# Four PSUM banks for the large products, one for the recurrence's first operand and its state update

## Chip, cores and metric

One core of one Trainium2 chip. The metric is device time in microseconds (us) of one execution. The kernel is written with tiles: the source sets no waits, they are derived from which instructions write and read a tile, and a tile with a tag takes one of the buffers of that tag (`bufs`, 1 where nothing is said). A buffer is taken again only when everything that used it has finished. PE, VectorE (DVE), ScalarE (ACT) and GpSimd (POOL) each run their own instructions in one fixed order.

## Reference

One layer over 1024 prompt tokens and 8 sample tokens (1032 columns, `TS`), width 2048, all in float32:

```python
mod = silu(c) @ w_ada + b_ada                     # shift, scale, gate
h = rmsnorm(x, norm_g) * (1 + sc) + sh
p_all = concat([shift_prev, h]) @ w_in            # 2048 x 10368
o_s, ... = s5_branch(u, z_s5, ...)                # state-space branch, GELU, GLU, SiLU(z)
o_r, wkv = rwkv_branch(cur, prev, z_rw, ...)      # 16 heads of 64; per token:
#   sa = S @ -kk;  S = S * d + outer(sa, b) + outer(v, k);  o = S @ r
#   then groupnorm, + sum(r * k * r_k) * v (bonus), times silu(z)
mixed = sigmoid(g_s5) * (o_s @ w_out[:1024]) + sigmoid(g_rw) * (o_r @ w_out[1024:])
y = rmsnorm(x + gt * mixed, final_g)
```

## The kernel before

Channels lie on partitions, tokens on the free axis. A large product is a *job*: 128 columns of a weight against all tokens, in three groups of some 344 tokens. Weights and activations are split into a high and a low float16 half, so one group is 3 x 16 matmuls (3 x 8 for the last weights) into one PSUM tile `pg` (L455, tag `g`, three banks). The group's evacuation by ScalarE and VectorE depends on the job: u L535, z of S5 (`zt`) L552/L553, r, k, v of the recurrence (`ZB`) and its low-rank input (`LW`) L511 to L517, z of the recurrence (`Z`) L567/L568, gates L587, output L1504. Next to it VectorE and ScalarE prepare the next job's weights: absolute maximum (L157), high half `whi` (L405), low half `wlo` (L406).

All other work is a set of Python generators that a driver (`Driver.slot`) steps between every eight matmuls, by estimated costs. This makes the order of the source; each engine's final order follows it, but an instruction whose inputs come late can stand behind later ones.

The recurrence (RWKV) runs over eight pairs of heads, 0 to 7, in chunks of 64 tokens. For each pair:
- `rw_prep` makes the decays and keys, with small products `pml` (L651) and `pmk` (L665) in the two `pm` banks; `rw_operands` makes the chunk matrices (`pma`, L737).
- `rw_side` transposes operands and makes the bonus term: three products `pmb` (L778), each read by VectorE (L779) into `BV`. Their tiles have the tags xp, sp, up. The jobs for the next pair's k and v need this step in the source's order, so it is issued at once ahead of them.
- `rw_tinv` inverts 16 triangular 64 x 64 matrices on VectorE by forward substitution, 63 steps of L798 and L800, writes the result to DRAM (`dT`, L804) and loads it back as `TT` (L808).
- `rw_chain` has 16 steps k. A step: `xp` = AR·S + M·VN (L826, L827); VectorE copies one half of the partitions to `XS` (L828), ScalarE the other to `XR` (L829); `up` = TT·XS (L834), VectorE makes `UB` of it (L835); `sp` = KN·VN + BN·UB (L837, L839); VectorE makes the next state `S` (L842); `up`'s second half (L840) and `XR` give the output `ON` (L845). xp, sp and up are a bank each.
- `rw_tail` normalizes and writes the pair's output to DRAM.

So the eight PSUM banks are: g 3, pm 2, xp, sp, up. The modulation products (`pmod` in `mod_block`, at the start; `pmg` in `gt_mod`, near the end) alternate over xp and sp, and the small transposing products behind them (`pmt`, `pmh`) use up. In the S5 stage `pmy` (L1290) needs `XRt`, a copy of the scan's states.

In PE's order the first step of a pair's chain begins early: L827 and L837 of k = 0 stand among the products for the next pair's v, and L834 of k = 0, which needs TT, behind those for its r.

Of the kernel before, what the change touches and what calls it, by code (L numbers as in the profile page):

```python
# [11 lines left out]
F32 = mybir.dt.float32  # L12
# [49 lines left out]
G3 = [(0, 344), (344, 688), (688, TS)]  # L62
# [68 lines left out]
class Hybrid:  # L131
# [79 lines left out]
    def mod_block(self, col, stage, row, out, xload=None):  # L211

        nc, d = self.nc, self.d
        self.mtog = 1 - getattr(self, "mtog", 0)
        q = self.ps.tile([128, 512], F32, name="pmod", tag=("xp", "sp")[self.mtog])
        for j in range(8):
            wa = stage(j)
            nc.sync.dma_start(wa, d["w_ada"][256 * j:256 * j + 256, col:col + 512].rearrange("(k p) n -> p k n", p=128))
            if xload is not None and j % 2:
                xload()  # L220
            self.mod_step(q, self.cs32, wa, 2 * j)
            yield (0, 600, 0)
        nc.scalar.copy(row, q)
        yield (0, 0, RGAP)
        q2 = self.ps.tile([128, 4, 16], F32, name="pmt", tag="up")
        for i in range(4):
            nc.tensor.matmul(q2[:, i, 0:9], row[:, 128 * i:128 * i + 128], self.sel, start=True, stop=True)
        out(q2)
        yield (300, 1000, 0)
# [197 lines left out]
    def run_jobs(self, jobs):  # L427

        nc, drv = self.nc, self.drv
        for i, job in enumerate(jobs):  # L430
            if job.need is not None:
                drv.force(lambda: job.need in self.flags)
            if job.before is not None:
                job.before()
            if job.bind is not None:
                job.bind()
            nxt = jobs[i + 1] if i + 1 < len(jobs) else None
            ws = None
            if nxt is not None:
                if nxt.ahead:  # L440
                    drv.force(lambda: nxt.known)
                ws = self.weights(nxt, jobs[i + 2] if i + 2 < len(jobs) else None)
                drv.bgs.insert(0, [ws, 0.0, 1.0])
            if i == 0:
                self.product_by_rows(job)
            for acc in job.accs if i else []:
                w_ = acc.job or job
                for g0, g1 in acc.groups:
                    q = self.ps.tile([128, 512], F32, name="pg", tag="g", bufs=3)
                    w = g1 - g0  # L450
                    n = 0
                    tot = 3 * len(acc.kts)
                    for wk, rk in acc.kts:
                        for a, b in ((w_.hi, acc.hi), (w_.hi, acc.lo), (w_.lo, acc.hi)):
                            nc.tensor.matmul(q[:, :w], a[:, wk, :], b[:, rk, g0:g1], start=(n == 0), stop=(n == tot - 1))  # L455
                            n += 1
                            if n % SLOT == 0 and n < tot:
                                drv.slot(SLOT * (w / 2.4 + 2.5))
                    v = acc.evac(q, g0, g1)
                    drv.slot(SLOT * (w / 2.4 + 2.5), v or 0.0)  # L460
            if nxt is not None:
                drv.force(lambda: getattr(nxt, "split", False))
            if job.done is not None:
                job.done()

    def product_by_rows(self, job):

        acc = job.accs[0]
        qs = [self.ps.tile([128, 512], F32, name="pg", tag="g", bufs=3) for _ in acc.groups]
        n = len(acc.kts)  # L470
        for i, (wk, rk) in enumerate(acc.kts):
            for q, (g0, g1) in zip(qs, acc.groups):
                for j, (a, b) in enumerate(((job.hi, acc.hi), (job.hi, acc.lo), (job.lo, acc.hi))):
                    self.nc.tensor.matmul(q[:, :g1 - g0], a[:, wk, :], b[:, rk, g0:g1], start=(i == j == 0), stop=(i == n - 1 and j == 2))
            self.drv.slot(1300, 0)
        for q, (g0, g1) in zip(qs, acc.groups):
            acc.evac(q, g0, g1)
# [274 lines left out]
    def rw_side(self):  # L752

        nc, c = self.nc, self.c
        V = nc.vector
        for p in range(8):
            while f"ops{p}" not in self.flags or (p and f"o{p - 1}" not in self.flags):
                yield None
            ON = self.ON.rearrange("p a t -> p (a t)")
            BV = self.BV[:, :T]  # L760
            n = 0
            for t, dst, W in ((5, self.BN, ON), (2, self.KN, BV), (7, self.VN, ON)):
                V.transpose(out=W, in_=self.z(t)[:, :T])
                yield (1150, 0, 0)
                W3 = W.rearrange("p (c b j) -> p c b j", c=16, b=2)
                for h in range(2):
                    for a in range(2):
                        for b in range(2):
                            p0 = 64 * h + 32 * a
                            d0 = 64 * h + 32 * b  # L770
                            f = nc.scalar.copy if n % 3 else nc.gpsimd.tensor_copy
                            f(dst[d0:d0 + 32, :, p0:p0 + 32], W3[p0:p0 + 32, :, b, :])
                            n += 1
                yield (0, 0, BGAP if t == 7 else 2000)
            RK, Vv = self.z(6), self.z(7)
            for (g0, g1), tag in zip(G3, ("xp", "sp", "up")):
                q = self.ps.tile([128, 512], F32, name="pmb", tag=tag)
                nc.tensor.matmul(q[:, :g1 - g0], c["bd"], RK[:, g0:g1], start=True, stop=True)  # L778
                V.tensor_tensor(out=self.BV[:, g0:g1], in0=q[:, :g1 - g0], in1=Vv[:, g0:g1], op=ALU.mult)  # L779
                yield (450, 578, PBG)  # L780
            nc.gpsimd.tensor_copy(self.SMP[:, 6, p, :], self.BV[:, T:TS])
            self.flags.add(f"side{p}")
# [29 lines left out]
    def rw_chain(self, p):  # L812
# [3 lines left out]
        for k in range(16):  # L816
# [4 lines left out]
            mb = self.M[:, k, 0:64] if e == 0 else self.M[:, k, 128:192]  # L821
            xs = self.XS[e]
            g = GC[:, k:k + 1]
            xp = self.ps.tile([128, 128], F32, name="xp", tag="xp")
            if k:
                nc.tensor.matmul(xp, self.AR[:, a, 128 * e:128 * e + 128], S0, start=True, stop=False)  # L826
            nc.tensor.matmul(xp, mk, self.VN[:, k, :], start=(k == 0), stop=True)  # L827
# [5 lines left out]
            up = self.ps.tile([128, 2, 128], F32, name="up", tag="up")  # L833
            nc.tensor.matmul(up[:, 0, :], self.TT[:, a, :], xs, start=True, stop=True)  # L834
            V.scalar_tensor_tensor(out=self.UB, in0=up[:, 0, :], scalar=-1.0, in1=c["bd"], op0=ALU.mult, op1=ALU.mult)  # L835
            sp = self.ps.tile([128, 128], F32, name="sp", tag="sp")
            nc.tensor.matmul(sp, self.KN[:, k, :], self.VN[:, k, :], start=True, stop=False)  # L837
            yield (200, 436, CG[1])
            nc.tensor.matmul(sp, self.BN[:, k, :], self.UB, start=False, stop=True)  # L839
# [510 lines left out]
    def gt_mod(self, st):  # L1350

        nc, d, c = self.nc, self.d, self.c
        V = nc.vector
        pool = self.pool("gtp", stack=st)
        small = lambda nm, *s, **k: pool.tile([128] + list(s), k.get("dt", F32), name=nm, tag=nm, bufs=k.get("bufs", 1))
        while "ysplit" not in self.flags:
            yield None
        cs32 = self.cond(pool)
        yield (300, 0, 2000)

        def load(n):
            w = []
            for h in range(2):
                t = self.ot.tile([128, 8, 128], F32, name="gw", tag="xres")
                nc.scalar.dma_start(t, d["w_ada"][1024 * h:1024 * h + 1024, 2 * DM + 128 * n:2 * DM + 128 * n + 128]
                                    .rearrange("(k p) n -> p k n", p=128))
                w.append(t)
            return w

        for n in range(16):  # L1370
            while n >= GQ and f"out{n - GQ}" not in self.flags:
                yield None
            w = load(n)
            yield (0, 0, 6000)
            q = self.ps.tile([128, 128], F32, name="pmg", tag=("xp", "sp")[n % 2])
            for h in range(2):
                self.mod_step(q, cs32, w[h], 8 * h)
            row = small("grow", 128)
            nc.scalar.copy(row, q)
            yield (0, 1300, 6000)  # L1380
            q2 = self.ps.tile([128, 16], F32, name="pmh", tag="up")
            nc.tensor.matmul(q2[:, 0:9], row, self.sel, start=True, stop=True)
            V.tensor_scalar(out=self.gt[:, n, :], in0=q2[:, 0:9], scalar1=c["b_ada"][:, 32 + n:33 + n], scalar2=None, op0=ALU.add)
            yield (200, 250, 0)
            self.flags.add(f"gt{n}")
            yield (0, 0, HGAP)
# [401 lines left out]
```

## Time and profile before

| | |
|---|---|
| median of 3 runs | 2989.96 us (2986.49 to 2994.73) |
| profiled execution | 2995.25 us |
| its span, first to last instruction | 2993.4 us |
| mean granted clock of TensorE | 0.961 of full speed |
| PE busy | 2735.1 us (91%) |
| VectorE busy | 2038.6 us (68%) |
| ScalarE busy | 1104.7 us (37%) |
| DMA, mean over the span | 101 GB/s |

A wait is the idle time of an engine just before an instruction, with what ended it. An engine's idle time costs only where the end of the kernel hangs on it. Matmuls overlap one another, so that one of 0.31 us takes PE some 0.145 us.

### The profile page before, as it was taken

What the parts mean: (1) busy time and instruction counts of PE and PEld (TensorE: products, weight loads), DVE (VectorE), ACT (ScalarE), POOL (GpSimd) and SP (SyncE); (2) the same over time, 40 slices, a digit from 0 to 9 for tenths busy, and PEclk for the clock granted to TensorE, in tenths of its full rate; (3) what the DMA queues carried; (4) which work ended last, traced back from release to release, by engine and by line L of the source; (5) the groups of instructions that cost most, each with busy time, mean ns of one, the idle gap of its engine ahead of it and who ended that gap; (6) DMA issues with size and microseconds to landing.
All of it is one profiled execution on the core that took longest, in us unless ns stands there. A gap on an engine that the chain in (4) does not pass through costs nothing.

```text
span 2993.4 us, 47028 instructions
## 1 busy us (share of the span) xinstructions
PE 2735.1 (91%) x18330; PEld 1819.5 (61%) x18330; DVE 2038.6 (68%) x5106; ACT 1104.7 (37%) x1934; POOL 189.8 (6%) x386
## 2 busy tenths in 40 slices
PE   5689989999989999899899899998999898999997
PEld 1156656666657666567566566575676665666664
DVE  5579788753676766855856856767667865656665
ACT  2143223333434344254254254253352145522321
POOL 1100000010100100000001001001000000000002
PEclk7799999999999999999999999999999999999998
DMA  9834443331321313123213212212222337574443
GB/s 334 270 73 90 88 71 92 95 87 49 65 63 48 81 51 78 52 64 82 57 44 77 71 47 74 60 52 66 62 72 70 106 131 258 164 239 142 141 142 128
DMA packets 434735, 301.82 MB, mean 101 GB/s; under 512 B 115184, under 2 KB 400016, under 8 KB 433232
## 3 DMA queue, kind: packets, MB, share of 16 engines
q1 hardware_dynamic: 398224, 281.19, 33.7%
q10 hardware_dynamic: 36128, 17.33, 2.1%
q8 instruction: 144, 2.36, 0.3%
q14 instruction: 79, 0.65, 0.1%
q0 software_dynamic: 160, 0.30, 0.0%
HBM read 241.44 MB, written 57.32 MB: 100 GB/s over the span
## 4 chain that ended last, share of the span: by engine, by line
PE 45%; DVE 26%; DMA 14%; issue 8%; ACT 4%; POOL 1%; SPq 1%; ACTq 0%; DVEq 0%; POOLq 0%
PE pg L455 33%; DMA ws<-w_in 4%; DMA od<-BV 4%; DVE TM L798 4%; DVE ZB L800 4%; DVE wlo L406 3%; PE pma L737 2%; DVE wam L157 2%; DMA wa<-w_ada 2%; PE up L840 1%; PE sp L839 1%; PE pmod L236 1%; PE up L834 1%; ACT whi L405 1%; DMA TT<-dT 1%
## 5 line engine op out<-in xcount | busy, mean ns | idle before, releaser
L455 PEld LDWEIGHTS <-whi 128*128 128x128 f16 x9600 | 945.5, 99 | 563.8 <-issue 113.0
L455 PE MATMUL pg<-H,whi 128*128 128x344 f16 (+2 forms) x3840 | 1202.2, 313 | 74.4 <-DVE ZB L517 42.7
L455 PE MATMUL pg<-H,wlo 128*128 128x344 f16 (+2 forms) x3840 | 1202.0, 313 | 0.0
L455 PE MATMUL pg<-HL,whi 128*128 128x344 f16 (+2 forms) x3840 | 1201.9, 313 | 0.0
L455 PEld LDWEIGHTS <-wlo 128*128 128x128 f16 x4800 | 474.2, 99 | 241.1 <-issue 16.3
L405 ACT ACTIVATE whi<-ws,wsc 128x512 f16<-128x512 f32 x404 | 267.4, 713 | 415.0 <-PE pg L455 147.3
L157 DVE TENSOR_REDUCE wam<-ws 128x1 f32<-128x512 f32 x404 | 267.0, 679 | 158.3 <-DMA ws<-w_in 112.9
L406 DVE SCALAR_TENSOR_TENSOR wlo<-ws,wsc,whi 128x512 f16<-128x512 f32 x404 | 292.6, 748 | 42.7 <-ACT whi L405 39.9
L455 PE MATMUL pg<-OH,whi 128*128 128x344 f16 (+3 forms) x960 | 297.9, 312 | 8.2 <-ACT OH L1432 6.2
L455 PE MATMUL pg<-OLo,whi 128*128 128x344 f16 (+3 forms) x960 | 299.1, 312 | 4.0 <-DVE OLo L1434 2.0
L455 PE MATMUL pg<-OH,wlo 128*128 128x344 f16 (+3 forms) x960 | 298.8, 312 | 0.5 <-DVE wlo L406 0.5
L798 DVE TENSOR_TENSOR TM<-ZB 128x252 f32<-128x252 f32 (+52 forms) x504 | 177.9, 353 | 97.2 <-DMA ZB<-c_t 87.0
L800 DVE TENSOR_TENSOR ZB<-ZB,TM 128x252 f32<-128x252 f32 (+52 forms) x504 | 178.5, 354 | 10.1
L154 POOL PARTITION_ALL_REDUCE wg<-wm x105 | 44.3, 422 | 1383.5 <-DVE wm L157 1344.8
L829 ACT COPY XR<-xp 64x128 f32<-64x128 f32 x128 | 33.1, 259 | 234.9 <-DVE XS L828 234.6
L236 PE MATMUL pmod<-wa,cs 128*32 128x512 f32 x256 | 77.6, 892 | 43.2 <-DMA wa<-w_ada 29.5
L831 ACT ACTIVATE SG<-S,GC 128x128 f32<-128x128 f32 x120 | 48.1, 401 | 151.8 <-DVE S L842 146.4
L1504 DVE SCALAR_TENSOR_TENSOR sg<-pg,oinv,sg 128x344 f32<-128x344 f32 (+3 forms) x96 | 54.9, 572 | 56.0 <-PE pg L455 55.7
L511 ACT ACTIVATE mt<-pg,rinv 128x347 f32<-128x347 f32 (+1 forms) x75 | 39.5, 537 | 136.2 <-PE pg L455 59.7
L842 DVE SCALAR_TENSOR_TENSOR S<-sp,GC,SG 128x128 f32<-128x128 f32 x120 | 41.7, 347 | 70.4 <-PE sp L839 68.0
L701 ACT COPY BT<-ZB 64x128 f32<-64x128 f32 x256 | 75.4, 296 | 34.4 <-PE pma L737 26.7
L834 PE MATMUL up<-XS,TT 128*128 128x128 f32 x256 | 54.9, 296 | 30.1 <-DMA TT<-dT 16.9
(449 smaller groups left out, 3128.3 us busy)
## 6 DMA issues: line engine op xcount, KB each, us to landing
ws<-w_in SPq DMA_DIRECT2D x162, 512.0 KB
wa<-w_ada SPq DMA_DIRECT2D x64, 512.0 KB
sg<-sgd SPq DMA_DIRECT2D x32, 516.0 KB
gw<-w_ada ACTq DMA_DIRECT2D x32, 512.0 KB
ws<-w_out SPq DMA_DIRECT2D x32, 512.0 KB
XT<-xT SPq DMA_DIRECT2D x16, 516.0 KB
xo<-xT SPq DMA_DIRECT2D x16, 516.0 KB
ZB<-dA SPq DMA_DIRECT2D x8, 1024.0 KB
```

What stands on the lines that cost most here:

```text
L157: self.nc.vector.tensor_reduce(out=out, in_=in_, axis=axis, op=ALU.max, apply_absolute_value=True)
L236: self.nc.tensor.matmul(q[s:s + 32], cs[:, kt, :], w[:, i, :], start=(kt < 4), stop=(kt >= 12))
L405: nc.scalar.activation(out=hi[:, ks, :], in_=s, func=AF.Copy, scale=job.sc[:, 0, 0:1])
L406: nc.vector.scalar_tensor_tensor(out=lo[:, ks, :], in0=s, scalar=job.sc[:, 0, 0:1], in1=hi[:, ks, :], op0=ALU.mult, op1=ALU.subtract)
L455: nc.tensor.matmul(q[:, :w], a[:, wk, :], b[:, rk, g0:g1], start=(n == 0), stop=(n == tot - 1))
L701: self.nc.scalar.copy(self.BT[k % 2][i][64 * h:64 * h + 64, :, 64 * h:64 * h + 64], t[64 * h:64 * h + 64, 128 * k:128 * k + 128].rearrange ...
L737: nc.tensor.matmul(q[:, e, 128 * i:128 * i + 128], w[:, e, :], self.AR[:, a, 128 * e:128 * e + 128], start=True, stop=True)
L798: nc.vector.tensor_tensor(out=TM, in0=row.unsqueeze(1).to_broadcast([128, n, m]), in1=TL[:, :n, k:k + 1].to_broadcast([128, n, m]), op=ALU ...
L800: nc.vector.tensor_tensor(out=TL[:, :n, k + 1:], in0=TL[:, :n, k + 1:], in1=TM, op=ALU.subtract)
L831: nc.scalar.activation(out=self.SG, in_=S0, func=AF.Copy, scale=g)
L834: nc.tensor.matmul(up[:, 0, :], self.TT[:, a, :], xs, start=True, stop=True)
L1504: V.scalar_tensor_tensor(out=f, in0=q[:, :g1 - g0], scalar=job.inv[:, w:w + 1], in1=f, op0=ALU.mult, op1=ALU.mult)
```

## The change

The tag `g` gets four buffers. xp and sp of a chain step become the halves of one tile `x2` (tag xs, 128 x 2 x 128 float32, half a bank). The other users of the tags xp, sp and up move: `pmod` and `pmg` alternate over xs and up, `pmt` and `pmh` go to the two `pm` banks, and the three bonus products use xs, up, xs. The banks are then g 4, pm 2, xs, up. No instruction is added or removed.

```diff
 mod_block:
-        q = self.ps.tile([128, 512], F32, name="pmod", tag=("xp", "sp")[self.mtog])
+        q = self.ps.tile([128, 512], F32, name="pmod", tag=("xs", "up")[self.mtog])
...
-        q2 = self.ps.tile([128, 4, 16], F32, name="pmt", tag="up")
+        q2 = self.ps.tile([128, 4, 16], F32, name="pmt", tag="pm", bufs=2)
 run_jobs:
-                    q = self.ps.tile([128, 512], F32, name="pg", tag="g", bufs=3)
+                    q = self.ps.tile([128, 512], F32, name="pg", tag="g", bufs=4)
 product_by_rows:
-        qs = [self.ps.tile([128, 512], F32, name="pg", tag="g", bufs=3) for _ in acc.groups]
+        qs = [self.ps.tile([128, 512], F32, name="pg", tag="g", bufs=4) for _ in acc.groups]
 rw_side:
-            for (g0, g1), tag in zip(G3, ("xp", "sp", "up")):
+            for (g0, g1), tag in zip(G3, ("xs", "up", "xs")):
 rw_chain:
-            xp = self.ps.tile([128, 128], F32, name="xp", tag="xp")
+            x2 = self.ps.tile([128, 2, 128], F32, name="xs", tag="xs")
+            xp, sp = x2[:, 0, :], x2[:, 1, :]
...
-            sp = self.ps.tile([128, 128], F32, name="sp", tag="sp")
             nc.tensor.matmul(sp, self.KN[:, k, :], self.VN[:, k, :], start=True, stop=False)
 gt_mod:
-            q = self.ps.tile([128, 128], F32, name="pmg", tag=("xp", "sp")[n % 2])
+            q = self.ps.tile([128, 128], F32, name="pmg", tag=("xs", "up")[n % 2])
...
-            q2 = self.ps.tile([128, 16], F32, name="pmh", tag="up")
+            q2 = self.ps.tile([128, 16], F32, name="pmh", tag="pm", bufs=2)
```

## Rows read from the trace of the kernel before

**Rows 1.** The page, busy time, share and instructions of each engine.
```profile
PE 2735.1 (91%) x18330; PEld 1819.5 (61%) x18330; DVE 2038.6 (68%) x5106; ACT 1104.7 (37%) x1934; POOL 189.8 (6%) x386
```

**Rows 2.** PE's waits: engine, waited for; us in total, times, longest us.
```profile
PE pg L455 <- DVE ZB L517: 42.7, 26, 3.1
PE pmod L236 <- DMA wa<-w_ada: 29.5, 26, 3.3
PE up L834 <- DMA TT<-dT: 16.9, 6, 3.6
PE pg L455 <- DVE Z L568: 16.5, 6, 4.3
...
PE up L834 <- DVE XS L828: 12.8, 9, 9.4
PE pg L455 <- DVE zt L553: 11.5, 2, 8.2
PE pml L651 <- ACT ZB L652: 10.1, 1, 10.1
```

**Rows 3.** PE's timeline, 427 to 642: start, us, instruction, [idle before <-releaser].
```profile
435.35 0.45 PE L455 MATMUL pg<-H,whi 128*128 128x344 f16 x1 [8.16 <-DVE zt L553]
...
471.87 0.82 PE L1290 MATMUL pmy<-XRt,CB 128*128 128x136 f32 x2 [5.11 <-ACT XRt L1283]
...
559.25 0.31 PE L455 MATMUL pg<-H,whi 128*128 128x344 f16 x1 [3.35 <-DVE zt L553]
...
641.87 0.31 PE L455 MATMUL pg<-H,whi 128*128 128x347 f16 x1 [1.30 <-DVE LW L517]
```

**Rows 4.** Tile pmb, 1618 to 1650: count, ns min/median/max, first and last start.
```profile
L778 PE MATMUL pmb<-ZB,c_mat x6: 452/452/453, 1622.0 to 1623.4; 128*128 128x344 f32 x6
L779 DVE TENSOR_TENSOR BV<-pmb,ZB x3: 506/507/509, 1642.0 to 1644.3; 128x344 f32<-128x344 f32 x3
```

**Rows 5.** PE's timeline, 1674 to 1705.
```profile
1676.05 0.38 PE L837 MATMUL sp<-VN,KN 128*128 128x128 f32 x2
...
1693.69 0.31 PE L455 MATMUL pg<-H,whi 128*128 128x346 f16 x1 [1.70 <-DVE ZB L517]
...
1704.20 0.77 PE L834 MATMUL up<-XS,TT 128*128 128x128 f32 x2 [3.31 <-DMA TT<-dT]
```

**Rows 6.** VectorE's timeline, 1688 to 1690.
```profile
1689.22 0.28 DVE L828 COPY XS<-xp 64x128 f32<-64x128 f32 x1
```

**Rows 7.** ScalarE's timeline, 1668 to 1693.
```profile
1689.54 0.26 ACT L829 COPY XR<-xp 64x128 f32<-64x128 f32 x1 [19.05 <-DVE XS L828]
```

**Rows 8.** Third pmb to end of first L779, six pairs: sum us, DVE busy.
```profile
sum 104.18, DVE 87.87; mean DVE 14.65
```

**Rows 9.** The longest waits of all engines, same columns as rows 2.
```profile
ACT XR L829 <- DVE XS L828: 234.6, 108, 20.2
```

**Rows 10.** First L837 to XR's end, six pairs: sum us, ACT busy.
```profile
sum 80.47, ACT 2.86; mean ACT 0.48
```

**Rows 11.** First L837 to first L834, six pairs: sum us, PE busy.
```profile
sum 170.18, PE 141.40; mean PE 23.57
```

**Rows 12.** Third pmb to first L837, six pairs: sum us, PE busy.
```profile
sum 308.90, PE 269.11; mean PE 44.85
```

**Rows 13.** Timelines of ScalarE and PE at two steps of one chain.
```profile
1714.23 0.26 ACT L829 COPY XR<-xp 64x128 f32<-64x128 f32 x1 [0.97 <-DVE XS L828]
...
1754.64 0.24 ACT L829 COPY XR<-xp 64x128 f32<-64x128 f32 x1
...
1714.25 0.49 PE L834 MATMUL up<-XS,TT 128*128 128x128 f32 x2
...
1752.50 0.38 PE L834 MATMUL up<-XS,TT 128*128 128x128 f32 x2
```

**Rows 14.** PE behind first L834, five pairs: stretch, us, busy (count), granted clock, DMA.
```profile
1495.23:1498.65 3.42, 3.42 (x15) 0.50 0.00 0
...
sum 23.15, PE 21.32; mean PE 4.26
```

## The prediction

> **What bounds the kernel now.** I read the busy shares first. PE is busy 2735.1 us, 91% of the span, and no other engine passes 68% [rows 1]. So a gain has to come out of PE's remaining idle time, and a loss is whatever adds to it. The second view is what ended PE's waits [rows 2]. A large product (`pg`) waits for its evacuation by VectorE behind lines L517, L568 and L553 for 42.7 + 16.5 + 11.5 us; with one wait of 1.30 us on LW [rows 3] that is 72.0 us. These are the bank waits: with three banks, group n starts only when group n-3 has been read. 72 us, 2.4%, is the most that a fourth bank can remove.
>
> The third step is where these waits lie. Three stand before the recurrence [rows 3]. Nearly all others lie in one stretch that comes once per head pair, while VectorE works through the triangular inverse (L798, L800). I take the pair at 1623 to 1704 us as the example; six pairs (1 to 6) look like it. PE issues the three bonus products `pmb` back to back from 1622.0, the last at 1623.4, but VectorE reads the first only at 1642.0 [rows 4]: it runs nearly 20 us behind. PE goes on with the products for k and v, with bank waits in between, does the first KN·VN of the new recurrence (L837) at 1676.05, does r's products with one bank wait more (1.70 us), and then sits 3.31 us in front of `up` (L834), which needs TT, the inverse come back from DRAM, at 1704.20 [rows 5]. VectorE copies XS at 1689.22 among the inverse's last steps [rows 6]; ScalarE, idle 19.05 us for it, then copies XR at 1689.54 for 0.26 us [rows 7]. So in this stretch VectorE sets the pace and PE waits for it somewhere in any case.
>
> **The change part by part.** *Four banks for `pg`.* This removes 72.0 us of waits, but not of time. In pairs 1 to 6, TT comes when the inverse is done; VectorE, nearly 20 us behind [rows 4], reads there only products that PE has finished. If PE's order stays, PE only reaches `up` sooner and waits longer there: gain 0. At 435.35 it could start 7 us earlier, but the next stop is `pmy` at 471.87, which already waits 5.11 us for ScalarE's XRt [rows 3], fed by VectorE: gain 0 (at most 2). The waits at 559.25 (3.35) and 641.87 (1.30) have no such stop until the recurrence's first operands: gain 4.65 us. In pair 0 PE later waits 10.1 us in `pml` for ScalarE [rows 2], which waits for the inverse: gain 0. In pair 7 the stop is `up` behind XS, 9.4 us [rows 2]: gain 0.
>
> *Bonus products on xs, up, xs.* The third `pmb` takes the bank of the first, so it must wait until VectorE has read the first. The three stand back to back on PE, and behind the third are all of k's, v's and r's products, since PE runs in order. From the third `pmb` to the end of that read is 104.2 us summed over pairs 1 to 6 [rows 8], 19.4 in the example. As PE had waits to lose in this stretch, this is not yet the loss.
>
> *xp and sp in one tile, so in one bank.* Now KN·VN (L837) writes a tile whose other half VectorE (XS) and ScalarE (XR) read. What the trace shows of such a tile: XR reads partitions that XS does not, and still it starts after XS ended, 108 times out of 128 [rows 9]. So accesses of two engines to one PSUM tile are put in sequence even where they don't overlap, and I take it that KN·VN will wait for XS and XR. No row shows PE as the second party.
> The Trainium skill ("PSUM — Partial Sum Buffer", section on bank collisions) says that two engines must not be in one bank and the same quadrant of partitions at once, whatever the columns, and that semaphores should guard by bank. KN·VN writes all 128 partitions, so by that rule it has to wait for both copies; the sequence of XR after XS in the trace is stricter than the rule, since those two are in different quadrants. By the rule the forecast below holds; without it the second rival does.
>
> For the first step (k = 0) of a pair the wait is long. KN·VN stands at 1676.05, in the midst of v's products, and XR ends at 1689.80: 13.75 us. r's products and then `up` are queued behind it. Over the six pairs, KN·VN to XR's end is 80.5 us [rows 10]; add 0.07 us each for the hand-over (an estimate from XS's end at 1689.50 to XR's start at 1689.54, and a little more for PE), 80.9. PE's own work from KN·VN to `up` is 141.4 us in 170.2 [rows 11]; in the example 23.1. So `up` comes 80.9 + 141.4 - 170.2 = 52.1 us later in all, 8.3 to 9.1 per pair; in the example 1689.87 + 23.1 = 1713.0 instead of 1704.2. The wait of the third `pmb` lies before this and mostly disappears in it: 1642.6 plus the PE work up to KN·VN (269.1 us over six pairs [rows 12], 44.4 in the example) gives 1687.0, still before 1689.87. Nothing behind `up` can take this back, since the chain, the next operands and the next inverse follow from it and the waits of rows 2 leave PE almost no other idle time: +52.1. In pair 0 KN·VN waits about 10 us too, but `pml` hides it (10.1 us of cover [rows 2]; without cover, +10). In pair 7 KN·VN stands just before `up`, which waits for XS anyway: +0.7, XR after XS.
>
> For the other 120 steps XR is usually ready in time: XR at 1714.23 for 0.26 us, while `up`, which stays ahead of KN·VN, runs at 1714.25 for 0.49 [rows 13]. In 14 steps ScalarE is late; the worst has `up` at 1752.50 and XR ending at 1754.88 [rows 13], about 2.1 us. If KN·VN stays right behind `up`, the 14 sum to 18.5 us; if it goes behind XR in PE's order, products fill the time and it is 0. No gain is possible, as KN·VN delays nothing now. In the four pairs with the worst case the order has room for 16 products before BN·UB, so I take 4, nearer the lower end.
>
> *Clock.* After a wait PE runs at the lower level: after `up` in five pairs the granted clock is 0.50, 1.2 GHz, for 23.15 us in all, with PE busy 21.3 [rows 14], so about 10.7 us are lost. Those waits at `up` vanish. But four of the KN·VN waits will be 2 to 3 us long, and after the wait at 1493.50, of 3.3 us, PE ran 3.42 us at 0.50 [rows 14], so I count 1.7 each, 6.8: net -3.9. The drop after the wait at `pmb` ends before KN·VN and is free.
>
> *The modulation tiles.* `pmod` still alternates over two banks and its stage waits for w_ada, 29.5 us [rows 2]; `pmt` and `pmh` get two banks where they had one. Cost 0; if `pm` were taken, at most a VectorE read of some 0.5 us for each of 24.
>
> The sum: 52.1 + 0.7 + 4 - 4.65 - 3.9 = +48 us against the profiled execution, 2995.25 us, 1.85 us of it outside the span of 2993.4. That run lies 5.3 us above the median of the three, 2989.96, so the median should become 2989.96 + 48 = 3038.
>
> **The rivals.** *Only the `pmb` wait.* KN·VN doesn't wait, because the halves are told apart. Then `up` comes at 104.2 + 0.4 + 269.1 + 141.4 - (308.9 + 170.2) = +36.0 us in six pairs (308.9 is `pmb` to KN·VN [rows 12]); with -4.65, and the clock about even (10.7 back at `up`, some 2 each lost behind `pmb`), +31: 3021. For it: no row shows PE held by such a tile. Against: XR behind XS.
>
> *Faster.* In the new program PE's order puts the third `pmb` and KN·VN behind the point where VectorE really arrives, say a group of products later, and `up` too. Then no new wait bites and the bank waits become progress: the idle time in six pairs is 308.9 - 269.1 + 170.2 - 141.4 = 68.6 us, of which 16.9 are waits for TT [rows 2], so -51.7 - 4.65 = -56: 2934. It decides itself at one place: where PE meets the third `pmb`, before or after VectorE's first L779. Against it: now PE is there 15 to 20 us too early, and the order is fixed in the program, with the third right behind the second.
> The Trainium skill ("Perfetto Trace Analysis", Optimization Strategy and Matmuls) holds that a gap that repeats on the busiest engine can mean too little PSUM and that products should rotate through banks; by that the 72 us would be the prize. The trace agrees that the gaps are bank waits, but not that PE is what the stretch waits for.
>
> *Same.* The new waits don't bite and the order stays: bank waits turn into waits for TT; only -4.65 remains, 2985, within 0.3%.
>
> *Worse steps.* The wait is as forecast, KN·VN stays right behind `up` in all steps (+14.5) and the clock gives nothing back (+3.9): 3056.
>
> **How the numbers follow.** Chances: forecast 0.66, only `pmb` 0.16, worse steps 0.08, same 0.05, faster 0.05. The range takes in the three slower cases with some microseconds beyond for the clock and the steps, 3008 to 3062; it leaves out about 0.15. A measurement here tells about 0.3% (9 us) from no change: slower 0.90, same 0.05, faster 0.05.
>
> **What would show it.** In the new profile PE should wait at `pmb` for VectorE's BV (L779), 14 to 19 us in six pairs, and at KN·VN (L837) for XR in pairs 0 to 7 at k = 0; `pg` should hardly wait for L517, L568 and L553; the waits of `up` for TT should be gone, with `up` some 8.8 us later after the inverse's end than now. The prediction is wrong if PE's order moves the third `pmb` by a group or more, if KN·VN shows no wait on ScalarE or VectorE, or if `up` still waits for TT.

## The result and the profile after

| | before | after |
|---|---|---|
| median | 2988.22 us (2976.02 to 2994.73, 4 runs) | 3075.87 us (3073.85 to 3077.95, 4 runs) |
| profiled execution | 2995.25 us, span 2993.4 | 3076.05 us, span 3074.2 |
| mean granted clock | 0.961 | 0.946 |

The changed kernel is slower: ratio 1.0283, 95% interval 1.0263 to 1.0303, or 88 us. The forecast was 3038 us with a range of 3008 to 3062. The direction is right, and the time lies above the range.

The page and PE's waits after, which answer to [rows 1] and [rows 2]:

```profile
PE 2742.0 (89%) x18330; PEld 1822.3 (59%) x18330; DVE 2033.9 (66%) x5106; ACT 1102.8 (36%) x1932; POOL 197.5 (6%) x386
```

```profile
PE pmb L778 <- DVE BV L779: 103.7, 8, 19.4
PE xs L837 <- ACT XR L830: 41.5, 17, 13.3
PE pmod L236 <- DMA wa<-w_ada: 31.5, 33, 4.1
PE pg L474 <- ACT H L359: 30.0, 1, 30.0
...
PE pg L455 <- ACT whi L405: 10.6, 3, 3.8
...
PE pg L455 <- DVE zt L553: 2.6, 1, 2.6
```

The bank waits behind L517 and L568 are gone and those behind L553 are nearly gone. In their place stand the two forecast waits, of `pmb` and of KN·VN (named xs now), and one that was not forecast: 30.0 us in one piece in front of the very first large products (L474), at the start of the kernel. Before, that wait was shorter:

```profile
153.26 1.02 PE L474 MATMUL pg<-H,whi 128*128 128x344 f16 x3 [9.48 <-ACT H L359]
```

Where the 80.8 us between the two traces lie, by the first product of each stage in each trace:

| stage | before, us | after, us | difference | forecast |
|---|---|---|---|---|
| start, to the second group of the second job | 186.9 | 213.3 | +26.4 | 0 |
| u and z of S5 | 421.4 | 416.9 | -4.5 | -4.65 with the next line |
| first gates, LW, k, v, r | 137.9 | 139.5 | +1.6 | |
| pair 0 | 229.2 | 225.6 | -3.6 | 0 |
| pairs 1 to 6 | 1262.3 | 1318.7 | +56.3 | +52.2 |
| pair 7 and the products after it | 240.7 | 240.6 | -0.1 | +0.7 |
| GLU | 127.7 | 130.9 | +3.2 | 0 |
| output | 387.4 | 388.8 | +1.4 | 0 |

A pair is counted from its z to the next one's; +52.2 is 52.1 + 4 - 3.9. The sums of the six windows, PE busy in them, before and after:

```profile
sum 1262.31, PE 1179.69; mean PE 196.62
```

```profile
sum 1318.65, PE 1186.13; mean PE 197.69
```

So the recurrence did about what was forecast, and the start is what the forecast missed. The profiled execution of before lay 7 us above the median, so that 80.8 us between the traces are 88 between the medians.

**The pairs.** PE's timeline of pair 4 after, which answers to [rows 5], and the rows of VectorE and ScalarE for [rows 6] and [rows 7]. In the new kernel the copies XS and XR and the product `up` stand one line lower (L829, L830, L835):

```profile
1690.10 1.51 PE L778 MATMUL pmb<-ZB,c_mat 128*128 128x344 f32 x2 [15.78 <-DVE BV L779]
...
1738.95 0.52 PE L837 MATMUL xs<-VN,KN 128*128 128x128 f32 x2 [4.30 <-ACT XR L830]
...
1763.34 0.39 PE L835 MATMUL up<-XS,TT 128*128 128x128 f32 x2
```

```profile
1738.24 0.28 DVE L829 COPY XS<-xs 64x128 f32<-64x128 f32 x1
```

```profile
1738.55 0.26 ACT L830 COPY XR<-xs 64x128 f32<-64x128 f32 x1 [9.35 <-DVE XS L829]
```

PE waits 15.78 us for VectorE's first L779, which stands at the same place among the inverse's rows as it did before. Then PE does the products, and at KN·VN it waits 4.30 us more, until 0.14 us after XR's end. `up` does not wait. It comes 24.4 us behind KN·VN, and PE is busy all that time.

**The start.** PE's timeline after:

```profile
136.39 1.06 PE L227 MATMUL pmt<-sel,mrow 128*128 128x9 f32 x8 [0.74 <-ACT mrow L223]
137.31 2.28 PE L294 MATMUL pst<-HL,ones 128*128 128x344 f32 x6
169.58 1.02 PE L474 MATMUL pg<-H,whi 128*128 128x344 f16 x3 [30.00 <-ACT H L359]
...
180.34 0.45 PE L474 MATMUL pg<-HL,whi 128*128 128x344 f16 x1 [9.46 <-DVE HL L360]
```

The product `pst` (L294) adds up the squares of x for the first rmsnorm. Before, it ran in the midst of the modulation products; here it stands right behind the last `pmt`. The tile `pst` before, and after it VectorE's timeline before and after, show what hung on it:

```profile
L294 PE MATMUL pst<-HL,ones x6: 452/453/557, 87.0 to 88.9; 128*128 128x344 f32 x6
```

```profile
101.67 11.72 DVE L301 TENSOR_TENSOR XT<-XT,RS 128x1032 f32<-128x1032 f32 x10
...
119.68 8.03 DVE L315 TENSOR_SCALAR XT<-XT,GS,SH 128x1024 f32<-128x1024 f32 x11
...
153.25 19.36 DVE L360 SCALAR_TENSOR_TENSOR HL<-XT,As,H 128x1032 f16<-128x1032 f32 x16 [0.62 <-ACT H L359]
```

```profile
149.13 18.38 DVE L301 TENSOR_TENSOR XT<-XT,RS 128x1032 f32<-128x1032 f32 x16
167.43 11.65 DVE L315 TENSOR_SCALAR XT<-XT,GS,SH 128x1024 f32<-128x1024 f32 x16
...
179.00 1.28 DVE L360 SCALAR_TENSOR_TENSOR HL<-XT,As,H 128x1032 f16<-128x1032 f32 x1
```

Before, VectorE normalized and modulated x (L301, L315) beside the modulation products, which wait for w_ada anyway. After, with `pst` 50 us later, these 18.38 + 11.65 us stand in one row behind the last modulation product, and the first low half of `H` comes at 179.00 instead of 153.25: 25.8 us. The delay behind the modulation is larger, 32 us, because in the trace of before the last `pmt` came 6.3 us later (143.5 against 137.2).

### The profile page after: what moved, and what is told of

Its sections match the earlier page's. It is cut to its first block, busy times and chain, and to the rows that moved or that the text cites. A ratio compares the mean times of both kernels' runs of the same rounds, so it can differ in the third digit from the quotient of the medians.

```text
span 3074.2 us, 46864 instructions
## 1 busy us (share of the span) xinstructions
PE 2742.0 (89%) x18330; PEld 1822.3 (59%) x18330; DVE 2033.9 (66%) x5106; ACT 1102.8 (36%) x1932; POOL 197.5 (6%) x386
## 4 chain that ended last, share of the span: by engine, by line
PE 37%; DVE 15%; DMA 11%; ACT 3%; issue 3%; POOL 1%; SPq 0%; ACTq 0%; DVEq 0%; POOLq 0%
PE pg L455 29%; DMA ws<-w_in 4%; DMA od<-BV 4%; DVE ZB L800 3%; DVE TM L798 3%; DVE wam L157 2%; DVE wlo L406 2%; PE pma L737 2%; PE up L840 1%; PE xs L839 1%; DMA ws<-w_glu 1%; PE up L835 1%; ACT whi L405 1%; PE xs L837 1%; PE xs L827 1%
## 5 line engine op out<-in xcount | busy, mean ns | idle before, releaser
L778 PE MATMUL pmb<-ZB,c_mat 128*128 128x344 f32 x48 | 22.2, 573 | 103.7 <-DVE BV L779 103.7
L830 ACT COPY XR<-xs 64x128 f32<-64x128 f32 x128 | 33.0, 258 | 170.1 <-DVE XS L829 169.8
L837 PE MATMUL xs<-VN,KN 128*128 128x128 f32 x256 | 54.5, 295 | 41.5 <-ACT XR L830 41.5
L842 DVE SCALAR_TENSOR_TENSOR S<-xs,GC,SG 128x128 f32<-128x128 f32 x120 | 41.6, 346 | 71.8 <-PE xs L839 70.9
```

## The experiments

Each line gives the median against the kernel before from the same set of runs, the ratio with its interval, and the sum over pairs 1 to 6 in the trace (before: 1262.3, and 1258.5 in the second trace, e5).

| run | against before, us | ratio | pairs 1 to 6, us |
|---|---|---|---|
| the change | +87.7 | 1.0283 [1.0263, 1.0303] | 1318.7 |
| e1 pmt, pmh back on up | +60.8 | 1.0206 [1.0188, 1.0225] | 1309.7 |
| e9 pst on g | +61.4 | 1.021 [1.0179, 1.0242] | 1318.5 |
| e2 e1, third pmb on pm | +48.2 | 1.017 [1.0147, 1.0193] | 1304.3 |
| e3 e1, KN·VN in up's tile | +43.2 | 1.0141 [1.011, 1.0172] | 1300.5 |
| e4 both | +26.4 | 1.0081 [1.0051, 1.011] | 1273.4 |
| e6 before, xp and sp in one tile | +51.6 | 1.0171 [1.0143, 1.0198] | 1308.9 |
| e7 before, third pmb on xp | +19.9 | 1.0062 [1.0041, 1.0084] | 1279.5 |
| e8 before, g 4 and pm 1 | +8.7 | 1.0033 [1.0017, 1.0049] | 1253.7 |
| e10 e4, later up | -4.9 | 0.9991 [0.9973, 1.001] | 1243.9 |
| e11 before, later up | -20.6 | 0.9933 [0.9914, 0.9952] | 1230.1 |
| e12 before, KN·VN in up's tile | +11.4 | 1.0044 [1.0029, 1.0058] | 1261.4 |

Every interval but that of e10 leaves out 1. Single traces of one program differ: e9 and e1 have the same pairs and differ by 9 us in them, and the median of the kernel before was 2979 to 2991 us in the sets. So differences below 10 us between the pairs of two traces are not read, and times in us that an expectation gives are compared by their distance from the kernel before.

**e1: the small modulation tiles back on up.**

```diff
-        q2 = self.ps.tile([128, 4, 16], F32, name="pmt", tag="pm", bufs=2)
+        q2 = self.ps.tile([128, 4, 16], F32, name="pmt", tag="up")
...
-            q2 = self.ps.tile([128, 16], F32, name="pmh", tag="pm", bufs=2)
+            q2 = self.ps.tile([128, 16], F32, name="pmh", tag="up")
```

> The changed kernel with one part undone: the small transposing products pmt and pmh are back in the bank up, so pst (the sums of squares, L294) has the two pm banks to itself again. Theory A (the start): in the changed kernel pst stood behind the last pmt, at 137.3 instead of 87.0 us, and the large products began 22 us late, a delay that never comes back. Then this kernel takes 3076 - 22 = 3054 us, pst stands near 87 us again, and PE's wait for H (L359) falls from 30.0 to about 9.5 us. Rival B (the forecast's zero for these tiles): the later start is swallowed by waits further on, and all the loss belongs to the recurrence; then it takes 3071 to 3076 us.

```profile
PE pg L474 <- ACT H L359: 9.2, 1, 9.2
```

The wait for H fell from 30.0 to 9.2 us, `pst` ran at 84.7 us, and 27 of the 88 us were gone (23 by the two ratios, where 22 were expected). Theory A holds, rival B falls: nothing later swallows the start's delay.

**e9: pst out of the pm banks, pmt left in them.**

```diff
-                q = self.ps.tile([128, 512], F32, name="pst", tag="pm", bufs=2)
+                q = self.ps.tile([128, 512], F32, name="pst", tag="g", bufs=4)
```

> The changed kernel with one line more: pst takes its three tiles from the four g banks, which are idle at that time; pmt and pmh stay in the pm banks. Theory A, made sharper: what delayed the start is that pst comes after the eight pmt in the source and now takes turns with them in the same two banks, so it may only start when the last pmt has been read. Then pst stands near 87 us again, the first large products begin near 153 us instead of 170, and the kernel is 0.7 to 0.9% faster than the changed one, as the first run of this set was: before x 1.020. Rival: pmt itself is slow in the pm banks, whatever pst does; then it stays at before x 1.028.

The tile `pst` in this run:

```profile
L294 PE MATMUL pst<-HL,ones x6: 781/781/940, 83.3 to 86.3; 128*128 128x344 f32 x6
```

The first products begin at 151.60 us, and the time is that of e1. So it is the sharing: `pst` comes behind the eight `pmt` in the source, and in common banks it has to take its turn behind them. `pmt` on the pm banks costs nothing by itself that these runs show.

**e6: only the shared tile, three banks.**

```diff
-            xp = self.ps.tile([128, 128], F32, name="xp", tag="xp")
+            x2 = self.ps.tile([128, 2, 128], F32, name="xs", tag="xp")
+            xp, sp = x2[:, 0, :], x2[:, 1, :]
...
-            sp = self.ps.tile([128, 128], F32, name="sp", tag="sp")
```

> The kernel before with one part of the change alone: xp and sp are the halves of one tile, everything else (three banks for pg, pmb on three banks, pmt and pmh on up) as it was. Theory C (the forecast's arithmetic): KN·VN at k = 0 waits 9 to 14 us for XR, and the six pairs take 52 us more; with the other steps and the clock before + 45 to 55 us. Rival F: what the wait costs is only what it cost between the two four-bank runs with and without it, 22 us in time and 31 us in the six pairs; then before + 22 to 31 us.

```profile
PE xs L837 <- ACT XR L830: 92.3, 17, 14.0
```

At k = 0 KN·VN waited 12.1 to 14.0 us in pairs 1 to 6, 79.8 in all (forecast 80.9), and the six pairs took 46.6 us more (50.4 against the second trace; forecast 52.1). Theory C holds, rival F falls.

**e7: only the third pmb, three banks.**

```diff
-            for (g0, g1), tag in zip(G3, ("xp", "sp", "up")):
+            for (g0, g1), tag in zip(G3, ("xp", "up", "xp")):
```

> The kernel before with the third pmb in the bank of the first (xp, up, xp) and nothing else. Theory C: PE waits 14 to 19 us in each of pairs 1 to 6, loses there its bank waits and its waits for TT, and the six pairs take 36 us more (the forecast's second case): before + 31 to 36 us. Rival G: with three banks the bank waits come back behind it, and the loss is nearer the whole wait, before + 50 us or more. Rival F: only the 17 us of time (27 us in the six pairs) that it cost between the four-bank runs with and without it.

```profile
PE pmb L778 <- DVE BV L779: 97.6, 8, 17.7
```

`pmb` waited 96.4 us in the six pairs (forecast 104.2), but the pairs took only 17 to 21 us more and the kernel 19.9. Rival F is nearest. The step behind C's 36 us was too dear: PE's idle time in the pairs grew by 26.3 us (108.95 - 82.62), and its busy time fell by 9.1 (1179.7 to 1170.6). Alone, the wait of `pmb` is much cheaper than that of KN·VN (19.9 against 51.6 us).

**e5: the kernel before, once more.**

> The kernel before, unchanged, for a trace from the same chip as the other runs of this set: in it the six pairs 1 to 6, from zr of pair 1 to zr of pair 7, should take 1262 us as in the first trace, and any difference to the first trace should lie in the start, where PE waits for transfers of w_ada.

The pairs took 1258.5 us and the start 181.6 instead of 186.9; `pst` ran at 84.3. The start is where the trace of before was long, but not by the waits for w_ada, which are longer here (46.2 us against 29.5): there the first modulation product began at 13.7 us, behind VectorE's copy of its operand (`cs`, L242), and here at 8.2.

**e2: e1 with the third pmb on pm.**

```diff
-            for (g0, g1), tag in zip(G3, ("xs", "up", "xs")):
-                q = self.ps.tile([128, 512], F32, name="pmb", tag=tag)
+            for (g0, g1), tag in zip(G3, ("xs", "up", "pm")):
+                q = self.ps.tile([128, 512], F32, name="pmb", tag=tag, bufs=2 if tag == "pm" else 1)
```

> As the run before it, and the third bonus product pmb in a pm bank, so that it waits for no L779. Only KN·VN still shares its bank with the recurrence's first operand. Theory C (the forecast's): the wait of pmb is nearly all swallowed by that of KN·VN. Then pmb's 103.7 us of waits go, the wait of KN·VN for XR at k = 0 grows from 4 or 5 us to 13 or 14 in six pairs (some 80 us), and the time stays within 6 us of the run before it (3048 to 3060). Rival D: the wait of pmb is itself the loss and KN·VN only takes what is left; then most of the loss goes and the time is 3000 us or less.

```profile
PE xs L837 <- ACT XR L830: 142.5, 17, 22.3
```

The waits of `pmb` went, and KN·VN's at k = 0 grew to 18.9 to 22.3 us, more than expected: with four banks PE reaches it sooner than with three (12.1 to 14.0 in e6). The six pairs took 5.4 us less, within what is not read; the median fell by 12.6, though the two intervals overlap. That is twice the 6 us that theory C allowed, and far from rival D, by which most of the loss would go: the wait of `pmb` is swallowed for the most part, perhaps not wholly.

**e3: e1 with KN·VN in up's tile.**

```diff
-            x2 = self.ps.tile([128, 2, 128], F32, name="xs", tag="xs")
-            xp, sp = x2[:, 0, :], x2[:, 1, :]
+            xp = self.ps.tile([128, 128], F32, name="xp", tag="xs")
...
-            up = self.ps.tile([128, 2, 128], F32, name="up", tag="up")
+            up = self.ps.tile([128, 3, 128], F32, name="up", tag="up")
+            sp = up[:, 2, :]
             nc.tensor.matmul(up[:, 0, :], self.TT[:, a, :], xs, start=True, stop=True)
+            nc.tensor.matmul(sp, self.KN[:, k, :], self.VN[:, k, :], start=True, stop=False)
             V.scalar_tensor_tensor(out=self.UB, in0=up[:, 0, :], scalar=-1.0, in1=c["bd"], op0=ALU.mult, op1=ALU.mult)
-            nc.tensor.matmul(sp, self.KN[:, k, :], self.VN[:, k, :], start=True, stop=False)
```

> As the first run, and KN·VN with BN·UB writes a third part of up's tile instead of a half of xp's; it stands right behind up in every step, k = 0 too, so that PE writes it into a bank that PE has just written. UB has to wait for it, some 0.2 us a step. The bonus products stay on xs, up, xs. Theory C: pmb's wait alone costs 31 to 36 us by the forecast's second case, so 3019 to 3024 us; up waits a few us for TT in the six pairs. Rival D: pmb is the whole loss; then it stays at 3048 to 3060. Rival E: without the wait of KN·VN nothing is left of the loss: 2990.

3022.1 us is the number of theory C, but against the kernel before of its set it is + 43.2 where C had 31 to 36; `pmb` waited 109.9 us, and `up` did not wait for TT. The edit itself costs 11 us on three banks (e12), which would make up the difference. D and E fall.

**e4: the edits of e2 and e3 together**: four banks, none of the three waits.

> Four banks for pg with none of the three new waits: pmt and pmh on up, the third pmb on pm, KN·VN and BN·UB in up's tile. The forecast's case of no bite: bank waits turn into waits of up for TT (some 68 us in six pairs), and only 4.65 us are gained: 2983 us, plus what the 0.2 us a step cost in the recurrence. Rival (the fourth bank is worth its bank waits): 2934 us, with few waits for TT.

```profile
PE up L835 <- DMA TT<-dT: 56.7, 6, 10.2
...
PE pml L651 <- ACT ZB L652: 18.0, 1, 18.0
PE pg L455 <- DVE ZB L517: 15.1, 13, 1.9
```

Most of the bank waits became waits of `up` for TT, in all six pairs, and nothing was gained: PE's idle time in the pairs is 88.2 us (1273.4 - 1185.2), before 82.6, and the kernel is 26.4 us slower than before, where the forecast's case of no bite said 5 faster. The rival's 2934 us falls.

**e8: four banks with one pm bank.** Every `tag="g", bufs=3` becomes 4 and every `tag="pm", bufs=2` becomes 1; nothing else.

> The fourth bank for pg without any of the three new waits: the kernel before with four buffers for g and one instead of two for pm; the recurrence's xp, sp and up and the bonus products keep a bank each. The forecast's case of no bite: bank waits turn into waits of up for TT, -4.65 us, plus what one pm bank costs its users (pml, pmk, pma and others; pmod and pmt are not among them): before - 5 to + 10 us. Rival: the fourth bank is worth its bank waits, before - 56 us.

The time is 8.7 us over before, inside the expected band. `pml` waits for ScalarE's ZB 60.3 us, 5.6 to 13.6 us in nearly every pair; pair 1 took 216 us instead of 207, pairs 4 to 6 took 205 to 207 instead of 211 to 213. But PE's order did not stay as it was: 50 to 55 large products more stand ahead of a pair's first `up` in pairs 1 to 6 (631 to 658, before 576 to 608). So this run has a later `up` too, which by e11 is worth something by itself, and doesn't give the price of the fourth bank alone.

**e12: KN·VN in up's tile, three banks** (the edit of e3 on the kernel before).

> The kernel before, three banks, with KN·VN and BN·UB in a third part of up's tile, as in the runs e3 and e4 (sp's own bank lies idle, except for pmb and pmod). It tells what of e4's before x 1.008 belongs to that edit. If the 0.2 us by which UB starts later in each step is what e4 lost, this run takes before + 10 to 25 us. If e4's surplus comes with the fourth bank (products that run ahead into waits for weights and operands), this run is within 9 us of before.

+11.4 us, at the low end of the first case. So of e4's 26 us some 11 would be this edit and some 15 come with the fourth bank, if the two add up, which was not tried. The trace doesn't place the 11 us: its pairs took 1261.4 us, like before.

**e10: e4 with a later up.** In pairs 1 to 6 the pause behind the chain's first step is longer:

```diff
-            yield (200, 436, CG[0])
+            yield (200, 436, CG[0] if k or p in (0, 7) else 9000)
```

> The run with four banks and none of the three new waits (e4), with the first up of pairs 2 to 6 put 61 products (some 9 us) later in PE's order by a longer pause behind the first step of the chain. If the bank waits that the fourth bank removes are given back as waits for TT only because up stands too early, the 56.7 us of waits for TT fall to some 10 (pair 1 is not moved) and the time to 3005 - 45 = 2960 us, before x 0.993 on that chip (1.0081 without the pause). Rival: VectorE sets the pace of the stretch whatever PE does, and the chain, begun later, ends later and holds up the bonus products and the inverse of the next pair; then it stays within 10 us of e4, and the waits turn up at pg or pml.

```profile
PE pml L651 <- ACT ZB L652: 53.3, 6, 15.6
PE pmod L236 <- DMA wa<-w_ada: 40.1, 27, 8.1
PE up L835 <- DMA TT<-dT: 21.1, 3, 11.9
```

0.9% faster than e4, some 27 to 31 of the 45 us. The waits for TT fell by 35.6 us; nearly all that is left of them lies in pair 1, where `up` didn't move, and in pair 7, where 11.9 us are new. `pml`'s waits for ScalarE's ZB rose by 35.3 us, to 6.8 to 8.1 us in each of pairs 2 to 6. Part of the stretch's idle time was only moved, as the rival says, and part became progress: PE's idle time in the pairs fell from 88.2 to 70.9 us.

**e11: the kernel before with a later up**, three banks; the edit of e10 with 8000 for 9000.

> The kernel before, three banks, with the same later up (62 products in pairs 2 to 6). The bank waits (72 us) stay; only the waits for TT, 16 us, can go. If four banks are what turns the later up into a gain, this one gains at most 14 us (before x 0.995); if the place of up is all that matters, it gains as much as the run with four banks does by it, some 45 us (before x 0.985).

2958.98 us, 20.6 us faster than before: the fastest kernel here, and it has three banks. The sum of its pairs:

```profile
sum 1230.08, PE 1166.87; mean PE 194.48
```

Most of its bank waits are still there (29.3 behind L517, 20.7 behind L568, 11.5 behind L553). Waits for TT are 17.3 us, of which 8.4 are new in pair 7; in the six pairs they fell from 16.9 to 8.9. The sum came down by 32 us, of which 19.4 are idle time of PE and 12.8 busy time. So four banks are not needed for the later `up` to pay: it gives 27 to 31 us with four (e4 to e10) and 20.6 with three, and the kernel with three ends 15.7 us ahead of e10. Both numbers of the expectation are missed, 14 and 45 us. In pairs 2 to 6 KN·VN of k = 0 moved along, by 56 to 64 products, where `up` moved by 52 to 62; which of the moved instructions gives the 20 us was not separated.

## Why the prediction was wrong

*The failed step is that of the modulation tiles*: "Cost 0; if `pm` were taken, at most a VectorE read of some 0.5 us for each of 24." It asked only what `pmt` and `pmh` would wait for. It did not ask who already used the pm banks at that time: `pst`, which follows all `pmt` in the source but ran ahead of them on PE, as long as the two used different banks. Put in turn with them, it ran 50 us later, and VectorE's 30 us of work on x lost the cover of the modulation products. The price is 25.8 us by VectorE's rows and 26.4 by the stage against the trace of before; against the second trace of before the stage is 31.7 us longer, and by the medians of e1 and e9 it is 26 to 27 us (22 to 23 by their ratios). Without it the time would be some 3049 to 3054 us, inside the range. The text ahead of the prediction had even named the rule by which `pst` had to wait, but the forecast applied it to `pmb`, and for the modulation tiles only to their own waits.

*Four banks for `pg`: right.* Of the 72.0 us of bank waits 2.6 are left, and the gain outside the pairs was 4.5 us in S5 (forecast 4.65 with the stage behind it, which lost 1.6). That the rest is only given back is what e4 shows (TT, 56.7 us). What came unforeseen is a small price: PE now runs into weights that are not ready, three waits for `whi`, 10.6 us in all, where before had one of 2.0. One of the three lies in GLU, which took 3.2 us longer. Small as they are, both stages repeat: S5 takes 416.9 to 419.5 us in the seven traces with four banks for g and two for pm, and 419.7 to 422.8 in the six with three. For GLU it is 130.4 to 132.4 and 127.7 to 130.8, so its price is less certain.
The Trainium skill ("Perfetto Trace Analysis", Optimization Strategy and Matmuls) says that such repeated gaps can mean too little PSUM, and has products rotate through banks. The gaps did go with more banks, but e4 and e8, each with one other change, were 26.4 and 8.7 us slower: the waits moved to other inputs.

*The third `pmb`: right in kind and nearly in size.* PE's order was kept; the third stands at most 12 products later. It waited 13.2 to 19.4 us in pairs 1 to 6, 96.3 in all, where 104.2 were forecast.

*KN·VN and the shared tile: right.* It waits for XR in pairs 0 to 6 at k = 0, and e6, where it stands alone, has 79.8 us of such waits against 80.9 forecast. Behind the wait of `pmb` 3.7 to 4.6 us of it remain in pairs 1 to 6 (2 to 3 forecast in four of them). In pair 7 it doesn't wait. The reading of XS and XR behind this step holds even further than the 108 waits said: in the trace of before XR starts behind XS's end in all 128 steps, at least 0.033 us later. That the wait of `pmb` is mostly swallowed is shown by the sums: shared tile alone +46.6 us (e6, three banks), both +47.3 (e1) or +56 (the change and e9), and by e1 against e2. `up` follows the inverse's end by 23.6 to 25.1 us in pairs 1 to 6, before by 13.0 to 14.0; forecast was 8.8 later, it is some 10.6.
The Trainium skill ("PSUM — Partial Sum Buffer", section on bank collisions) asks for semaphores by bank and quadrant; a wait of PE for both copies is what it would lead to, and the trace agrees. Whether the wait goes by bank or by tile was not tried.

*Other steps: 4 us forecast, about nothing found.* Outside k = 0 the longest wait of KN·VN for XR is 0.34 us, and the waits of all 17 but the seven at k = 0 sum to 2.8 us.

*Clock: mis-sized.* Forecast was -3.9 us: 10.7 back behind `up`, 6.8 lost behind four waits of KN·VN. Three windows of after, behind `pmb`, behind KN·VN and behind `up`, in that order (stretch, us, busy, granted clock, DMA):

```profile
1690.10:1693.50 3.40, 3.40 (x10) 0.50 0.02 5
1738.95:1742.40 3.45, 3.45 (x13) 0.54 0.39 86
1763.34:1766.90 3.56, 3.56 (x26) 1.00 0.00 0
```

Behind `up`, where PE had not waited, nothing is lost any more, as forecast: the granted clock in the 7 us behind it is 1.00 in all six pairs. Behind `pmb` and KN·VN it is at or near 0.50, 1.2 GHz. The stretch behind `pmb` lies ahead of the wait at KN·VN and is free. Behind KN·VN the loss comes in all six pairs and not in four: the granted clock in the 7 us behind it is 0.57 to 0.76, which makes 13.4 us lost, twice the forecast (the missing share of the full clock times 7 us, over the six pairs; in e1 the clock is 1.00 once and 0.76 else, and 8.4 us are lost). So the term was some +2.7 us here and -2.3 in e1. It can't be read from PE's busy time in the pairs, which rose by 6.4 us (1179.7 to 1186.1) and by 1.1 in e1, because the free stretch is in it too.

With these sizes the pairs come to 52.1 + 0 + 2.7 = 54.8 us, and 56.3 were measured. That the forecast's 52.2 lies so near is partly luck, because the terms for the steps and for the clock missed in opposite directions.

*The rivals.* "Only the `pmb` wait" (3021) falls: KN·VN does wait. Its own price was too high as well, +36 in the pairs against 17 to 21 in e7. "Same" and "faster" fall with e4. "Worse steps" falls with the 0.34 us, though its other half, a clock that gives nothing back, is nearer than the forecast here.

## What to carry to other kernels

Before a tile is moved to another bank, list all who take turns in that bank, in the order of the source: a late product that used to run ahead of early ones will have to queue behind them. Count a bank wait as a gain only after finding the next input that PE would wait for; here 72 us of them were worth at most 5. Where waits only change places, move the instruction that stands too early: the first KN·VN and `up` of a chain, some 60 products later, gave 20.6 us with no bank added.

## What was not expected of the hardware

Nothing of the chip itself came out otherwise than the traces of before let one think. One size was new: PE started 0.14 us after the end of the ScalarE copy that it waited for (1738.55 + 0.26 to 1738.95), twice the 0.07 us estimated, and so in all six pairs.
